# A hybrid encoder in fp32: a prologue ordered by channel tiles, and lower weight parts made by an accumulating transfer

## The chip, the cores and the metric

The kernel runs on one core of a Trainium2 chip. The metric is device time in microseconds (us) of one execution; a kernel's time is the median of its runs. The engines are TensorE (PE in the profile; its weight loads PEld), VectorE (DVE), ScalarE (ACT), GpSimd (POOL) and SyncE (SP). SP's queue issues most of the loads; GpSimd and ACT can issue transfers from queues of their own.

## The reference

Two layers, each a token mixer and a gated MLP, on x of shape (1, 256, 1024), all in float32:

```
for i in range(DEPTH):                                   # DEPTH = 2
    h = rms_norm(x, norm_mix_pre[i])
    u_hy, q, k, v, g_out, gate_lr, u_pool, gate_logits = split(h @ w_in[i])
    y_hy   = hyena_mixer(u_hy, ...)      # depthwise conv, long convolution by FFT, gating
    y_gla  = gla_mixer(q, k, v, g_out, gate_lr, ...)     # gated linear attention, both directions
    y_pool = pool_mixer(u_pool, ...)     # centred means over 2, 4, 8, 16, then a small matmul
    gates  = sigmoid(gate_logits)
    merged = gates[0] * (y_hy @ w_br_hyena[i]) + gates[1] * (y_gla @ w_br_gla[i]) \
           + gates[2] * (y_pool @ w_br_pool[i])
    x = x + rms_norm(merged @ w_out[i], norm_mix_post[i])
    h = rms_norm(x, norm_ffn_pre[i])
    a, b = split(h @ ffn_w_up[i])
    x = x + rms_norm((gelu(dwconv3(a)) * b) @ ffn_w_down[i], norm_ffn_post[i])
```

## The kernel before

**Precision by parts.** Each float32 operand of a matmul is written as an upper part, the value rounded to the format fp32r, and a lower part, the value minus the upper one. A product is three matmuls that add up in PSUM: upper by upper, upper by lower, lower by upper (`mm3`). For weights, ACT makes the upper part by a copy (`act`, line 106) and VectorE the lower one by a subtraction (`tt`, line 111).

**Weights.** They come in 71 chunks of 128x2048 a layer, with one small chunk between them, in a fixed order; chunk n is position n. `dma_next` loads the next chunk from SP's queue into one of three buffers (`raw`). `split_upper` and `split_lower` each turn half a chunk (128x1024) into a buffer of the pool `b` (37 buffers of 4 KB a partition). When the second half's lower part is asked for, the raw buffer is given back and the next load is written down. So the load of one chunk waits for the split of an earlier one. Some chunks ("paired", line 195) are loaded as two transfers. Chunks 10 to 23 are, in the first layer: the second chunk of the Hyena branch's x0, two of q, two of the pooling branch, two of k, then gates and projection of the pooling branch, and the first gate chunk of the Hyena branch.

**Order.** The program is written as a sequence of units, each a group of matmuls with its evictions; between units, `filler` splits further half chunks, up to three chunks ahead, as far as `b` has free buffers. Side generators (Hyena filters, attention heads, the pool products, which write `y_pl`) step in between. Tile's scheduler then orders the instructions on each engine by its own simulation of time. Every engine works through its own queue in order; a buffer's next user waits for the last user of what it held.

**The prologue** is under a manual schedule, in which the order of the code is kept. The token rows come in two tiles, x of tile 0 and of tile 1. For each: half of the squares on ACT, half on VectorE (`squares`), mean on VectorE and power -1/2 on GpSimd (`rstd_mean`), scaling (`scaled`), eight transposes (`turned`), then copies out of PSUM times the norm's gain, with upper and lower part (`gained`, by bank of two channel tiles). The gains in a column come from `grow`, a load of 8x128. `upper(k)` and `lower(k)` split a quarter of weight chunk 0, of 512 columns.

Of the kernel before, what the change touches and what calls it, by code (L numbers as in the profile page):

```python
# [16 lines left out]
ALU = mybir.AluOpType  # L17

P = 128
DEPTH = 2  # L20
L = 256
DM = 1024
# [62 lines left out]
def trunk(ctx: ExitStack, tc: tile.TileContext, a: dict, out: bass.AP):  # L85
    nc = tc.nc
# [8 lines left out]
    def f32(ap):  # L95
        return ap.bitcast(F32)
# [8 lines left out]
    def act(o, i, func=AF.Copy, **kw):  # L105
        ins = nc.scalar.activation(o, i, func, **kw)  # L106
        if func in TABLED:
            tc.stamp_issue_order_token(ins.ins, TOKEN)

    def tt(o, x, y, op):  # L110
        nc.vector.tensor_tensor(out=o, in0=x, in1=y, op=op)  # L111

    def stt(o, x, s, y, op0=ALU.mult, op1=ALU.mult):
        nc.vector.scalar_tensor_tensor(out=o, in0=x, scalar=s, in1=y, op0=op0, op1=op1)  # L114
# [42 lines left out]
    def load_x(t, parts):  # L157
        for s in parts:
            nc.sync.dma_start(xs[t][:, s], a["x"][t * P:(t + 1) * P, s])  # L159
# [8 lines left out]
    load_x(0, HALVES)  # L168
    gcol = cpool.tile([P, 8], F32, name="gcol")
    grow = cpool.tile([8, P], F32, name="grow")  # L170
    nc.sync.dma_start(grow[:], a["gains"][0, 0].rearrange("(k c) -> k c", c=P))


    order = []
# [5 lines left out]
    raws, wh, wl = {}, {}, {}  # L180
    state = {"dma": 0, "h": 0, "l": 0}

    def dma_next(parts=1, between=None):
        n = state["dma"]
        if n >= len(order):
            return
        kind, c = order[n]
        w = 2048 if kind == "w" else 512
        r = wpool.tile([P, w], F32, tag="raw", name=f"raw{n}")
        src = a["wts"][c] if kind == "w" else a["lrw"][c]  # L190
        if kind == "w" and c % NCHUNK in PAIRED:
            side = (c % NCHUNK - 16) % 3
            for m in range(2):
                src = a["wts"][c - side + m][:, side * 1024:(side + 1) * 1024].rearrange("p (k c) -> p k c", c=256)
                nc.sync.dma_start(r[:].rearrange("p (k c) -> p k c", c=512)[:, :, m * 256:(m + 1) * 256], src)
            parts = 0
        for m in range(parts):
            s = slice(m * w // parts, (m + 1) * w // parts)
            nc.sync.dma_start(r[:, s], src[:, s])
            if between is not None and m == 0:  # L200
                between()
        raws[n] = r
        state["dma"] = n + 1

    def split_upper():
# [13 lines left out]
        wl[n].append(big.get([P, 1024], F32R))  # L219
        act(wh[n][half][:], raws[n][:, half * 1024:(half + 1) * 1024])  # L220

    def split_lower():
        n, half = divmod(state["l"], 2)
        state["l"] += 1
        if order[n][0] == "lr":
            if half == 0:
                t = wh[n][0]
                r = raws[n][:].rearrange("p (k c) -> p k c", k=8)
                tt(t[:, :, 1, 0:32], r[:, :, 0:32], f32(t[:, :, 0, 0:32]), ALU.subtract)
        else:  # L230
            tt(wl[n][half][:], raws[n][:, half * 1024:(half + 1) * 1024], f32(wh[n][half][:]), ALU.subtract)
        if half == 1:
            del raws[n]
            dma_next()

    def split_half(lead=True):

        if state["l"] >= 2 * len(order):
            return
        if state["h"] == state["l"]:  # L240
            split_upper()
        if lead and state["h"] == state["l"] + 1 and state["h"] // 2 in raws and len(big.free) >= ahead["reserve"] + 4:
            split_upper()
        split_lower()
# [5 lines left out]
    def weights(n, at, width):  # L250

        half, at = divmod(at, 1024)
        return wh[n][half][:, at:at + width], wl[n][half][:, at:at + width]

    dma_next(2, lambda: load_x(1, [slice(0, DM)]))
    dma_next(2)
    dma_next()
    nc.sync.dma_start(vec[:], a["vec"])
# [123 lines left out]
    def rstd_mean(ss):  # L382

        r = cpool.tile([P, 1], F32, tag="rstd", bufs=4, name="rstd")
        e = cpool.tile([P, 1], F32, tag="mse", bufs=4, name="mse")
        tsc(e[:], ss[:, 0:1], ss[:, 1:2], EPS, ALU.add, ALU.add)
        nc.gpsimd.tensor_tensor(out=r[:], in0=e[:], in1=mhalf[:, 0:1], op=ALU.pow)  # L387
        return r
# [887 lines left out]
    def squares(t):  # L1276
        h, ss = big.get([P, DM]), ssq_tile()
        s0, s1 = HALVES
        act(h[:, s0], xs[t][:, s0], AF.Square, scale=1.0 / 32.0, accum_out=ss[:, 0:1])
        x = xs[t][:, s1]  # L1280
        nc.vector.scalar_tensor_tensor(out=h[:, s1], in0=x, scalar=1.0 / 1024.0, in1=x, op0=ALU.mult, op1=ALU.mult,
                                       accum_out=ss[:, 1:2])
        return h, ss

    def scaled(t, h, r):
        s0, s1 = HALVES
        act(h[:, s1], xs[t][:, s1], scale=r[:, 0:1])
        for s in (slice(s0.start, s0.start + 256), slice(s0.start + 256, s0.stop)):
            nc.vector.tensor_scalar_mul(h[:, s], xs[t][:, s], r[:])

    def turned(h):
        ps = [psm.get([P, 2, P]) for _ in range(4)]
        for k in range(8):
            nc.tensor.transpose(ps[k // 2][:, k % 2, :], h[:, k * P:(k + 1) * P], ident[:])  # L1294
        big.put(h)
        return ps

    def gained(t, half, ps, banks=(0, 1)):
        s = slice(t * P, (t + 1) * P)
        for bank in banks:  # L1300
            b = ps[half * 2 + bank]
            of = [(xt[0][half][:, k, s], xt[1][half][:, k, s], b[:, k % 2, :], gcol[:, half * 4 + k:half * 4 + k + 1])
                  for k in (2 * bank, 2 * bank + 1)]
            for xh, _, src, g in of:
                act(xh, src, scale=g)
            for xh, xl, src, g in of:
                stt(xl, src, g, f32(xh), ALU.mult, ALU.subtract)
            psm.put(b)
# [4 lines left out]
    def upper(k):  # L1313
        act(wh[0][k // 2][:, k % 2 * 512:(k % 2 + 1) * 512], raws[0][:, k * 512:(k + 1) * 512])

    def lower(k):
        s = slice(k % 2 * 512, (k % 2 + 1) * 512)
        tt(wl[0][k // 2][:, s], raws[0][:, k * 512:(k + 1) * 512], f32(wh[0][k // 2][:, s]), ALU.subtract)
# [14 lines left out]
    ps0 = turned(h0)  # L1333
# [2 lines left out]
    gained(0, 0, ps0, (0,))  # L1336
    upper(1)
    lower(1)
    gained(0, 0, ps0, (1,))
    h1, ss1 = squares(1)  # L1340
    r1 = rstd_mean(ss1)
    for k in (2, 3):
        upper(k)
        lower(k)
    scaled(1, h1, r1)
    del raws[0]
    dma_next()
    state["h"] = state["l"] = 2
# [158 lines left out]
```

## Time and profile before

| | |
|---|---|
| median of 3 runs | 886.82 us (885.36 to 887.30) |
| profiled execution | 885.61 us, of which the span is 883.8 us |
| TensorE busy | 871.4 us, 99% of the span |
| VectorE, ACT, GpSimd busy | 635.8, 511.8, 37.9 us |
| TensorE's granted clock | 0.998 |
| bytes moved by DMA | 163.46 MB, mean 185 GB/s |

The profile is that of one execution. A row of its timeline has the start in us from the span's start, the duration in us, the engine, the line of the kernel, the operation and its tiles (out<-in), and in brackets how long the engine was idle ahead of it and what ended that. L106 is the helper through which all ACT work goes, L111 that of VectorE's tensor-tensor operations, L120 that of matmuls; there one goes by the names of the tiles. A row of the waits has an engine, whom it waited for, the sum in us, how often, and the longest. A row by stretch of time has the stretch, its length, then the busy time of PE, PEld, DVE, ACT and POOL with the number of instructions, then the granted clock, the DMA engines' busy share and GB/s.

### The profile page before, as it was taken

The page shows a single profiled execution, that of the slowest core. Times are in us where ns is not written, and L with a number is a line of the kernel's source. Part 1 is how long each engine was busy: PE and PEld are TensorE (multiplying, and loading weights), DVE is VectorE, ACT ScalarE, POOL GpSimd, SP SyncE. Part 2 cuts the span into 40 slices and gives each one's busy share as a digit, 9 for nine tenths or more (in the row PEclk, how much of TensorE's full clock was granted, in tenths as well). Part 3 has the DMA queues.
Part 4 walks back from the last instruction along what each step waited for, and adds up shares of the span by engine and source line. Part 5 has one row for each costly group of instructions (what it writes and reads, how often), then busy time and mean ns, then how long its engine had stood idle before and what let it go on. Part 6 is the DMA issues. An engine that isn't in the chain of part 4 may idle for free.

```text
span 883.8 us, 13488 instructions
## 1 busy us (share of the span) xinstructions
PE 871.4 (99%) x5381; PEld 782.4 (89%) x5381; DVE 635.8 (72%) x925; ACT 511.8 (58%) x809; POOL 37.9 (4%) x86
## 2 busy tenths in 40 slices
PE   8999999999999999999999999999999999999996
PEld 6899987888888999998889999888888899999885
DVE  6899989766586798665288989876755967776612
ACT  6778757555365776554267855864543665555501
POOL 3000100000010000000010000000000000000000
PEclk9999999999999999999999999999999999999999
DMA  8863625746546436466349453455752674455501
GB/s 287 325 233 131 215 96 190 240 145 238 191 159 246 143 134 248 149 221 224 121 136 349 161 164 131 153 195 179 279 184 78 239 281 144 168 170 207 195 1 48
DMA packets 48143, 163.46 MB, mean 185 GB/s; under 512 B 3410, under 2 KB 29157, under 8 KB 33232
## 3 DMA queue, kind: packets, MB, share of 16 engines
q1 hardware_dynamic: 44080, 151.70, 48.9%
q0 software_dynamic: 4000, 10.90, 3.8%
q8 instruction: 42, 0.69, 0.3%
q14 instruction: 21, 0.17, 0.1%
HBM read 161.54 MB, written 1.05 MB: 184 GB/s over the span
## 4 chain that ended last, share of the span: by engine, by line
PE 95%; DVE 2%; DMA 1%; ACT 1%; issue 0%; SPq 0%; DVEq 0%; POOLq 0%; ACTq 0%
PE p L120 93%; DMA raw<-in_wts 1%; DVE b L111 1%; ACT b L106 1%; PE p L374 1%; PE p L1059 0%; PE p L1204 0%; PE p L775 0%; PE p L1021 0%; PE p L876 0%; DVE s L111 0%; PE p L1294 0%; SPq L159 0%; DVE x L114 0%; DVEq L1503 0%
## 5 line engine op out<-in xcount | busy, mean ns | idle before, releaser
L120 PE MATMUL p<-b,b 128*128 128x256 f32 (+2 forms) x5022 | 840.1, 328 | 4.0 <-DVE b L111 2.3
L120 PEld LDWEIGHTS p<-b,b 128*128 128x128 f32 x5022 | 739.8, 190 | 86.6 <-DVE b L111 3.7
L111 DVE TENSOR_TENSOR b<-raw,b 128x1024 fp32r<-128x1024 f32 (+2 forms) x288 | 342.3, 1208 | 114.1 <-ACT b L106 59.6
L106 ACT ACTIVATE b<-raw 128x1024 fp32r<-128x1024 f32 (+2 forms) x290 | 292.2, 1041 | 161.2 <-PE p L120 127.4
L111 DVE TENSOR_TENSOR b<-p,b 128x512 f32<-128x512 f32 (+2 forms) x72 | 45.8, 655 | 66.1 <-ACT s L106 44.6
L106 ACT ACTIVATE b<-p 128x512 f32<-128x512 f32 (+3 forms) x90 | 50.0, 571 | 64.2 <-PE p L120 38.7
L106 ACT ACTIVATE s<-p 128x256 f32<-128x256 f32 (+3 forms) x50 | 20.3, 415 | 69.0 <-PE p L120 68.7
L114 DVE SCALAR_TENSOR_TENSOR s<-p,vec,s 128x255 f32<-128x255 f32 x104 | 49.4, 479 | 6.5 <-ACT s L106 5.5
L106 ACT ACTIVATE s<-p,vec 128x256 f32<-128x256 f32 x52 | 28.8, 557 | 18.1 <-DVE s L114 15.5
L106 ACT ACTIVATE s<-s 128x512 f32<-128x512 f32 (+6 forms) x54 | 28.9, 535 | 11.5 <-DVE s L111 5.6
L111 DVE TENSOR_TENSOR b<-s,b 128x512 fp32r<-128x512 f32 (+1 forms) x42 | 28.6, 686 | 6.0 <-ACT b L106 6.0
L106 ACT ACTIVATE b<-s 128x512 fp32r<-128x512 f32 x38 | 23.5, 625 | 9.2 <-DVE s L111 9.1
L111 DVE TENSOR_TENSOR b<-b,b 128x512 f32<-128x512 f32 (+4 forms) x28 | 22.4, 802 | 3.6 <-ACT b L106 3.1
L111 DVE TENSOR_TENSOR b<-b,p 128x512 f32<-128x512 f32 x24 | 16.2, 683 | 7.7 <-PE p L120 7.3
L111 DVE TENSOR_TENSOR s<-s,p 128x512 f32<-128x512 f32 x22 | 15.0, 684 | 8.4 <-ACT s L106 8.0
L106 ACT ACTIVATE b<-b,s 128x128 f32<-128x128 f32 x64 | 20.5, 392 | 0.4 <-DVE s L700 0.4
L114 DVE SCALAR_TENSOR_TENSOR b<-p,vec,b 128x255 f32<-128x255 f32 (+1 forms) x40 | 19.1, 478 | 0.4 <-ACT b L106 0.3
L387 POOL TENSOR_TENSOR rstd<-mse,mhalf 128x1 f32<-128x1 f32 x16 | 9.3, 581 | 210.5 <-DVE mse L117 210.5
L106 ACT ACTIVATE b<-p,vec 128x256 f32<-128x256 f32 (+1 forms) x24 | 12.6, 527 | 9.0 <-PE p L120 7.1
L106 ACT ACTIVATE b<-b 1x512 f32<-1x512 f32 (+3 forms) x16 | 12.5, 783 | 4.2 <-DVE b L111 4.1
L106 ACT ACTIVATE s<-x 128x512 f32<-128x512 f32 x12 | 7.6, 634 | 11.6 <-DVE x L114 11.4
L111 DVE TENSOR_TENSOR s<-b,b 128x512 f32<-128x512 f32 x20 | 13.1, 685 | 1.5 <-PE p L120 1.4
(108 smaller groups left out, 310.7 us busy)
## 6 DMA issues: line engine op xcount, KB each, us to landing
raw<-in_wts SPq DMA_DIRECT2D x116, 1024.0 KB, 4.8
raw<-in_wts SPq DMA_DIRECT2D x52, 512.0 KB, 5.3
b<-in_gains POOLq DMA_DIRECT2D x7, 512.0 KB, 4.5
b<-in_dft POOLq DMA_DIRECT2D x4, 512.0 KB, 6.9
b<-in_gw POOLq DMA_DIRECT2D x2, 512.0 KB, 5.5
b<-in_fw POOLq DMA_DIRECT2D x2, 512.0 KB, 7.3
b<-in_decay POOLq DMA_DIRECT2D x2, 512.0 KB, 7.3
out<-x SPq DMA_DIRECT2D x4, 256.0 KB, 2.0
```

The lines of the kernel that those rows point to most:

```text
L106: ins = nc.scalar.activation(o, i, func, **kw)
L111: nc.vector.tensor_tensor(out=o, in0=x, in1=y, op=op)
L114: nc.vector.scalar_tensor_tensor(out=o, in0=x, scalar=s, in1=y, op0=op0, op1=op1)
L120: ins = nc.tensor.matmul(o, w, x, start=start, stop=stop).ins
L374: nc.tensor.transpose(ps[k // 4][:, k % 4, :], h[:, k * P:(k + 1) * P], ident[:])
L387: nc.gpsimd.tensor_tensor(out=r[:], in0=e[:], in1=mhalf[:, 0:1], op=ALU.pow)
```

## The change

Four edits:

- The load of `grow` is issued from ACT's queue instead of SP's.
- Chunk 0 is loaded in four quarters instead of two halves; x's tile 1 still goes when half of them are issued.
- In the prologue, the squares and the mean of x's tile 1 stand ahead of the second `gained` of tile 0; upper and lower part of quarter 3 stand around the scaling of tile 1.
- For the second half of chunks 10 to 23, `split_lower` has ACT write minus the raw weights, rounded to fp32r, and a transfer from GpSimd's queue add the raw weights to it.

```diff
-    nc.sync.dma_start(grow[:], a["gains"][0, 0].rearrange("(k c) -> k c", c=P))
+    nc.scalar.dma_start(grow[:], a["gains"][0, 0].rearrange("(k c) -> k c", c=P))
...
-            if between is not None and m == 0:
+            if between is not None and 2 * m + 2 == parts:
                 between()
...
+    def by_dma(n, half):
+        return 10 <= n < 24 and half == 1
+
     def split_lower():
...
+        elif by_dma(n, half):
+            src = raws[n][:, half * 1024:(half + 1) * 1024]
+            act(wl[n][half][:], src, scale=-1.0)
+            nc.gpsimd.dma_start(wl[n][half][:], src, accum_op=ALU.add)
         else:
             tt(wl[n][half][:], raws[n][:, half * 1024:(half + 1) * 1024], f32(wh[n][half][:]), ALU.subtract)
...
-    dma_next(2, lambda: load_x(1, [slice(0, DM)]))
+    dma_next(4, lambda: load_x(1, [slice(0, DM)]))
...
     lower(1)
-    gained(0, 0, ps0, (1,))
     h1, ss1 = squares(1)
     r1 = rstd_mean(ss1)
-    for k in (2, 3):
-        upper(k)
-        lower(k)
+    gained(0, 0, ps0, (1,))
+    upper(2)
+    lower(2)
+    upper(3)
     scaled(1, h1, r1)
+    lower(3)
     del raws[0]
```

In the rows of order below a name's numbers are the buffer's and the tile's own. VectorE's queue in the prologue of the kernel before, from the lower part of chunk 0's second quarter on (`b_5` to `b_8` are parts of chunk 0, `b_1` and `b_3` x's parts, `b_10` the rows of tile 1):

```order
L111 TENSOR_TENSOR b_7_111<-raw_81,b_5_109 128x512
L114 SCALAR_TENSOR_TENSOR b_3_105<-p_4_140,gcol,b_1_103 128x128 x2
L1281 SCALAR_TENSOR_TENSOR b_10_163,ssq<-x_68 128x512
L117 TENSOR_SCALAR mse<-ssq 128x1
L111 TENSOR_TENSOR b_8_112<-raw_81,b_6_110 128x512 x2
L1289 TENSOR_SCALAR b_10_163<-x_68,rstd 128x256 x2
L114 SCALAR_TENSOR_TENSOR b_3_105<-p_8_202,gcol,b_1_103 128x128 x2
```

And in the changed kernel:

```order
L111 TENSOR_TENSOR b_7_113<-raw_81,b_5_111 128x512
L1288 SCALAR_TENSOR_TENSOR b_10_161,ssq<-x_68 128x512
L117 TENSOR_SCALAR mse<-ssq 128x1
L114 SCALAR_TENSOR_TENSOR b_3_107<-p_4_142,gcol,b_1_105 128x128 x2
L111 TENSOR_TENSOR b_8_114<-raw_81,b_6_112 128x512
L1296 TENSOR_SCALAR b_10_161<-x_68,rstd 128x256 x2
L111 TENSOR_TENSOR b_8_114<-raw_81,b_6_112 128x512
L114 SCALAR_TENSOR_TENSOR b_3_107<-p_8_204,gcol,b_1_105 128x128 x2
```

The squares and mean of tile 1 now stand ahead of a gain step, and the last lower part of chunk 0 behind the scaling.

GpSimd's queue in the first layer, before, from the memsets behind the load of the inverse DFT (`b_110`) to the load of the attention's norm gains:

```order
L813 MEMSET b_110_1375 1x256
L814 MEMSET b_110_1375 1x64x2
L815 MEMSET b_110_1375 1x256
L914 MEMSET b_117_1422 128x2
L609 DMA gn<-in_glan 128x128
```

And now (raw_1106, 1257, 1152, 1348, 1515, 1591 and 1626 are chunks 17, 19, 18, 20, 21, 22 and 23):

```order
L820 MEMSET b_110_1385 1x256
L821 MEMSET b_110_1385 1x64x2
L822 MEMSET b_110_1385 1x256
L236 DMA b_106_1340<-raw_1106 128x1024
L921 MEMSET b_117_1432 128x2
L236 DMA b_124_1519<-raw_1257 128x1024
L236 DMA b_120_1449<-raw_1152 128x1024
L236 DMA b_129_1594<-raw_1348 128x1024
L236 DMA b_133_1630<-raw_1515 128x1024
L236 DMA b_138_1687<-raw_1591 128x1024
L236 DMA b_143_1734<-raw_1626 128x1024
L616 DMA gn<-in_glan 128x128
```

The transfers of chunks 17 to 23 stand in that stretch, chunk 19's ahead of chunk 18's. Those of chunks 10, 11, 13 and 12 stand ahead of the second DFT load, those of 14, 15 and 16 between the load of the pool weights and that of the inverse DFT.

ACT's queue before, from the first upper part of chunk 21 (raw_1504) to the second pool copy (`b_115`; `b_125` are copies out of PSUM for the Hyena products; raw_1579 is chunk 22):

```order
L106 ACTIVATE b_130_1609<-raw_1504 128x1024
L106 ACT_TABLE_LOAD
L106 ACTIVATE b_125_1511<-p_51_1512 128x512
L106 ACTIVATE b_115_1416<-p_50_1493,vec 128x256
L106 ACTIVATE b_135_1665<-raw_1579 128x1024
L106 ACTIVATE b_125_1511<-p_52_1552 128x512
L106 ACTIVATE b_132_1616<-raw_1504 128x1024
L106 ACTIVATE b_115_1416<-p_50_1493,vec 128x256
```

And now (`b_133` is minus the upper part of chunk 21's second half, raw_1515):

```order
L106 ACTIVATE b_130_1621<-raw_1515 128x1024
L106 ACTIVATE b_133_1630<-raw_1515 128x1024
L106 ACTIVATE b_115_1426<-p_50_1503,vec 128x256
L106 ACTIVATE b_132_1629<-raw_1515 128x1024
L106 ACT_TABLE_LOAD
L106 ACTIVATE b_125_1522<-p_51_1523 128x512
L106 ACTIVATE s_37_1609<-b_97_1214 1x512
L106 ACTIVATE s_42_1860<-b_49_445,s_7_447 128x128 x2
L106 ACTIVATE b_115_1426<-p_50_1503,vec 128x256
L106 ACTIVATE b_125_1522<-p_52_1563 128x512
```

Ahead of it, minus the upper part of chunk 19 stands right behind the first upper part of that chunk, and the second upper part comes later. The table load and the copies `b_125` moved behind both parts of chunk 21.

## The prediction

> **What bounds the kernel now.** I read the engines' busy time first, then the chain that ended last, then what TensorE (PE) waited for, then the table by stretch of time.
>
> ```profile
> PE 871.4 (99%) x5381; PEld 782.4 (89%) x5381; DVE 635.8 (72%) x925; ACT 511.8 (58%) x809; POOL 37.9 (4%) x86
> ...
> PE 95%; DVE 2%; DMA 1%; ACT 1%; issue 0%; SPq 0%; DVEq 0%; POOLq 0%; ACTq 0%
> ```
> ```profile
> PE p L120 <- DVE b L111: 2.3, 2, 1.8
> PE p L120 <- ACT b L106: 1.8, 2, 1.4
> PE p L120 <- DVE rmask L260: 1.2, 1, 1.2
> PE p L1294 <- DVE b L1289: 0.4, 1, 0.4
> ```
> ```profile
> 60.00:90.00 30.00, 30.00 (x237) 29.02 (x237) 29.90 (x62) 25.60 (x54) 1.87 (x6) 1.00 0.32 125
> 90.00:120.00 30.00, 30.00 (x232) 29.04 (x231) 27.13 (x47) 20.07 (x40) 2.51 (x8) 1.00 0.49 159
> 120.00:150.00 30.00, 28.22 (x127) 23.09 (x126) 27.08 (x40) 18.96 (x30) 0.00 (x0) 1.00 0.53 175
> ```
>
> TensorE is the bound. All its waits (us in total, times, longest) add up to 5.7 us: the start, and one wait of 1.8 us, which takes TensorE to 28.22 of 30 us in the last stretch. VectorE (DVE) is busy 29.90 of 30 us from 60 to 90 us, yet TensorE is at 30.00 there: taking work off VectorE shortens nothing by itself. What can be gained is a piece of the start, and the wait of 1.8 us; what can be lost is any cover that keeps TensorE dense.
>
> **The start.** Rows of the timeline (start, duration, then the work; in brackets the idle time before it), the first from the chain:
>
> ```profile
> 2.06 5.95 DMA raw<-in_wts
> ...
> x<-in_x SPq DMA_DIRECT2D x1, 512.0 KB, 6.8
> ...
> 2.46 0.43 SPq L159 DMA_DIRECT2D x<-in_x  x1
> ...
> 8.04 0.63 ACT L106 ACTIVATE b<-raw 128x512 fp32r<-128x512 f32 x1 [1.37 <-DMA raw<-in_wts]
> ...
> 10.95 0.68 DVE L1281 SCALAR_TENSOR_TENSOR b<-x 128x512 f32<-128x512 f32 x1
> ...
> 11.75 0.21 DVE L117 TENSOR_SCALAR mse<-ssq 128x1 f32<-128x1 f32 x1
> 11.88 1.28 DVE L111 TENSOR_TENSOR b<-raw,b 128x512 fp32r<-128x512 f32 x2
> 13.08 0.61 DVE L1289 TENSOR_SCALAR b<-x,rstd 128x256 f32<-128x256 f32 x2
> ...
> 12.04 0.93 POOL L387 TENSOR_TENSOR rstd<-mse,mhalf 128x1 f32<-128x1 f32 x1 [6.12 <-DVE mse L117]
> ...
> 13.48 1.20 PE L1294 MATMUL p<-ident,b 128*128 128x128 f32 x8 [0.37 <-DVE b L1289]
> ```
>
> The second half of x lands at 2.46 + 6.8 = 9.26 us, but VectorE squares its part of it only at 10.95, behind two lower parts and two gain steps. From there the mean (11.75), the power on GpSimd (12.04 to 12.97), the scaling (13.08) and the transposes (13.48) follow. The change loads the first weight chunk in quarters, with x between the second and the third. The bytes ahead of x are the same but for the 4 KB of gains, which go to ACT's queue, ahead of its table load; I cost both at nothing, since x's landing is set by the bytes queued before it. The first quarter lands earlier than 8.02 us: ACT's idle 1.37 us shrinks, and upper and lower parts 0 and 1 are out of the way by x's landing. Squares then run from about 9.3 to 10.0, mean by 10.2, power by 11.15. On VectorE there follow the gain step (two, 0.6) and lower part 2 (0.69, half of the row of 1.28), whose upper part ACT makes by 11.1; so VectorE reaches the scaling at about 11.8 instead of 13.08. The gain of lower part 3's move behind the scaling is in this. Transposes at 12.3 instead of 13.48: **1.2 us** gained. Bounds: 0.3 if x or the third quarter lands a microsecond later, since four smaller transfers stand in the same queue; 1.9 if scaling waits for the power alone (11.15 against 13.08).
>
> **Fourteen lower parts by a transfer.** Chunks 10 to 23 are meant, the second half of each.
>
> ```profile
> L111 DVE TENSOR_TENSOR b<-raw,b 128x1024 fp32r<-128x1024 f32 (+2 forms) x288 | 342.3, 1208 | 114.1 <-ACT b L106 59.6
> L106 ACT ACTIVATE b<-raw 128x1024 fp32r<-128x1024 f32 (+2 forms) x290 | 292.2, 1041 | 161.2 <-PE p L120 127.4
> ...
> raw<-in_wts SPq DMA_DIRECT2D x116, 1024.0 KB, 4.8
> ...
> b<-in_gains POOLq DMA_DIRECT2D x7, 512.0 KB, 4.5
> ```
> ```profile
> b<-in_gw POOLq DMA_DIRECT2D x1, 512.0 KB, 3.6
> ```
> ```profile
> b<-in_dft POOLq DMA_DIRECT2D x1, 512.0 KB, 8.5
> ```
>
> VectorE loses 14 x 1.21 = 16.9 us, ACT gains 14 x 1.04 = 14.6 us. Neither sum is on the path, but ACT runs in order: at 25.60 of 30 us from 60 to 90 us, four or five more parts fill it. I cost that at nothing there, since ACT has 9.9 us free in the next stretch, and price the order of its work below, where it matters.
>
> The accumulating transfer has no row. The nearest are plain loads of 512 KB from the same queue (last column: us from issue to landing): 3.6 with the DMA engines quiet, 4.5 at the median of the seven gains, 8.5 for one at 76 us. It also reads its destination; from 512 KB (3.6) to 1024 KB (4.8, on SP's queue) another 512 KB took 1.2 us. So I take 4.5 + 1.2 = **5.7 us**, with ends 3.6 (the second read is free) and 8.5 + 1.2 = 9.7 us. I choose near the median because SP's row below has no weight load issued between chunk 20's pair (from 103.47) and chunk 21's pair (its second at 121.77), where the price decides.
>
> The Trainium skill, "DMA: Bandwidth & Descriptors", section "Anatomy of one DMA — SWDGE (gpsimd) path", gives about 2.0 us plus the bytes at 436 GB/s; its page "Collectives: The Full Stack", section "The bandwidth ceiling: the fold count and why AG ≠ RS ≠ AR", says that an add in a transfer costs a second source read rather than cycles. By both, as an estimate, the price is 2.0 + 1.2 + 1.2 = 4.4 us, and the sum below would be +0.55 instead of +1.85; the plain rows here (4.5 at the median, against 3.2 by the formula) speak for more.
>
> **Where it meets the path.** A raw buffer used to be free when VectorE had made the second lower half; now it is free when the transfer has landed. Three raw buffers stand behind this, so each of SP's loads 13 to 27 starts later against its split, and the transfers queue on GpSimd, in whose order a DFT load, the pool weights, the inverse-DFT loads and memsets stand behind transfers that wait for ACT. I cost that at nothing: each is held by a negation of 1.04 us or two, and TensorE works on other branches meanwhile. Most loads have cover too. The place without is the wait of 1.8 us: chain, then ACT's rows there, then the rows ahead of it.
>
> ```profile
> 121.77 5.37 DMA raw<-in_wts
> ...
> 127.16 1.07 ACT b L106
> ...
> 128.25 1.23 DVE b L111
> ...
> 131.68 4.69 DVE b L111 x6
> ...
> 136.41 3.70 PE p L120 x15
> ```
> ```profile
> 128.24 1.28 ACT L106 ACT_TABLE_LOAD   x1
> 129.53 0.60 ACT L106 ACTIVATE b<-p 128x512 f32<-128x512 f32 x1
> 130.03 0.47 ACT L106 ACTIVATE b<-p,vec 128x256 fp32r<-128x256 f32 x1
> ...
> 131.81 1.07 ACT L106 ACTIVATE b<-raw 128x1024 fp32r<-128x1024 f32 x1
> 132.76 0.48 ACT L106 ACTIVATE b<-p,vec 128x256 fp32r<-128x256 f32 x1
> 133.12 0.62 ACT L106 ACTIVATE s<-b 1x512 f32<-1x512 f32 x1
> 133.64 0.68 ACT L106 ACTIVATE s<-b,s 128x128 f32<-128x128 f32 x2
> ```
> ```profile
> 103.47 18.80 SPq L195 DMA_DIRECT2D raw<-in_wts  x4
> ...
> 110.83 0.47 ACT L106 ACTIVATE b<-p,vec 128x256 fp32r<-128x256 f32 x1 [2.13 <-PE p L120]
> ...
> 116.23 2.96 ACT L106 ACTIVATE b<-raw 128x1024 fp32r<-128x1024 f32 x3 [2.78 <-PE p L120]
> ```
>
> Chunk 21's load is a pair: SP's row ends at 122.27, its last issue is the chain's 121.77, and the one ahead of it, as long, starts near 121.35. It lands at 127.14; ACT's upper part, VectorE's lower part, the Hyena products and then the lower part of chunk 20 follow, and TensorE waits for that last one until 136.41. In the new order the buffer for chunk 21 comes from chunk 19's transfer. ACT makes minus the upper part of chunk 19 right behind that chunk's first upper part, which waits for TensorE to free a buffer until 116.23. With TensorE 1.2 earlier, the negation ends between 112.2 (right behind the pool copy at 110.83 less 1.2, its 0.47 and two parts) and 117.1 (behind 116.23 less 1.2 and two parts). I take 116.1, near the upper end, since buffers come free with TensorE's progress and the new form holds them no shorter. Plus 5.7 the load is issued at 121.8. To keep pace with a TensorE that is 1.2 earlier it had to go at 120.15: **1.65 us** late. The ends of the transfer's price give −0.45 and 5.65.
>
> Then ACT's order behind chunk 21's first upper part. Before, the first copy out of PSUM for the Hyena products started 2.4 us after that part (129.53 against 127.16), the second pool copy 5.6 us after it. Now minus the upper part of chunk 21 (1.05), a pool copy (0.47) and chunk 21's second upper part (1.07) stand between it and the table load: the first copy moves back by some 2.1 us, and the second pool copy, for which TensorE's pool products wait, by 0.6 (a short row and the two 128x128 pieces also pass it, another copy and a chunk's upper part leave). I take **1.4 us**, the middle, since VectorE has the lower part and a product of older data to do meanwhile; ends 0 and 2.1.
>
> **The sum**: −1.2 + 1.65 + 1.4 = +1.85 us on the profiled execution's 885.61, which lies 1.2 under the median of the runs, 886.82. So 888.7 us by the runs.
>
> **The rivals.** *Not slower: a quick transfer.* At 3.6 us chunk 21's load goes at 119.7, 0.45 ahead of need. If ACT's new order is also hidden (0), the wait shrinks from 1.8 to 1.35 and the start's 1.2 stays: −1.65, and −2.35 with the start's 1.9, so 884.5 to 885.2. The mechanism is the early release of one raw buffer; it decides from a landing under 4.05 us after the issue. The 3.6 row speaks for it, the second operand against it.
>
> *Slow transfers.* The plain load at 76 us took 8.5 us with VectorE full (29.90 of 30) and the DMA engines at 0.32. At 9.7 us the sum is −1.2 + 5.65 + 1.4 = +5.85, so 892.7, and transfers queued behind each other (chunks 19, 18 and 20 follow in one row on GpSimd's queue) could make a second place like it: 897. TensorE would then wait already for chunks' own lower halves. For it: VectorE is at 27 of 30 us from 90 to 150 us too. Against: it loses the fourteen products there, and the same queue brought the gains in 4.5. The Trainium skill, "SBUF — State Buffer", section "SBUF: two separate sides", says that VectorE's two-port operations keep GpSimd from writing descriptors, so that such transfers seem blocked; by that rule the 8.5 would be the price wherever VectorE is full. The trace shows the slow load but not its cause.
>
> *The start gives nothing.* If the quarters delay x by as much as the order saves (gain 0.3), the loss is 2.75: 889.6.
>
> **Chances.** The likeliest case 0.48, its own range 886.5 to 890.5; the quick transfer 0.22; slow transfers 0.20; no gain at the start 0.10. A change under 0.2%, 1.77 us, is about what a measurement of this kernel cannot tell from none. The likeliest case lies at that edge (888.6) and is split 0.24 same, 0.24 slower; the quick one 0.15 faster, 0.07 same; slow transfers all slower; the last 0.07 same, 0.03 slower; rounded: faster 0.15, same 0.38, slower 0.47. The range, 885.2 to 896, leaves out the better half of the quick case and the end of the slow one.
>
> **What the profile after would show.** Right: transposes near 12.3; fourteen transfers from raw to b on GpSimd's queue at about 5.7 us each; chunk 21's load issued at 121 to 122.5; TensorE's wait near 133 us grown from 1.8 to about 4.8 us, with chunk 21's landing behind it, and TensorE dense elsewhere; VectorE 17 us lighter, ACT 15 heavier. Wrong: landings near 3.6 or 9; new waits between 60 and 130 us, of TensorE for b from a transfer; transposes still at 13; or the wait gone although chunk 21 comes as late, which would say that VectorE's queue made it.

## The result: 1.2% slower, and the profile after

| | before | after |
|---|---|---|
| median of runs | 886.09 us (4 runs, 884.21 to 887.30) | 896.26 us (4 runs, 895.36 to 897.77) |
| span of the profiled execution | 883.8 us | 895.0 us |

The ratio of the times is 1.0119 (95% interval 1.0105 to 1.0133): 10.2 us lost, where 1.9 were forecast; 896.26 lies just above the range (885.2 to 896.0). The profiled executions differ by 11.2 us, and two views of the kernel after hold that sum within 0.3 us. Its engines' busy time and TensorE's waits:

```profile
PE 875.9 (98%) x5381; PEld 784.8 (88%) x5381; DVE 622.1 (70%) x911; ACT 523.4 (58%) x823; POOL 49.7 (6%) x100
...
PE p L120 <- DMA b<-raw: 7.9, 3, 4.5
PE p L120 <- ACT b L106: 3.1, 2, 2.0
PE p L120 <- DVE rmask L267: 1.2, 1, 1.2
PE p L1301 <- DVE b L1296: 0.5, 1, 0.5
```

The waits are 12.7 us against 5.7, which is 7.0 more; and TensorE is busy 4.5 us longer with the same 5381 matmuls. The timeline shows where the waits lie; these are the rows from 10 us on that TensorE idled before:

```profile
10.94 1.52 PE L120 MATMUL p<-b,b 128*128 128x512 f32 x3 [1.12 <-ACT b L106]
...
134.37 15.82 PE L120 MATMUL p<-b,b 128*128 128x512 f32 x62 [4.49 <-DMA b<-raw]
...
152.21 6.36 PE L120 MATMUL p<-b,b 128*128 128x512 f32 x26 [2.01 <-ACT b L106]
159.42 3.02 PE L120 MATMUL p<-b,b 128*128 128x512 f32 x12 [0.85 <-DMA b<-raw]
168.68 6.46 PE L120 MATMUL p<-b,b 128*128 128x512 f32 x25 [2.60 <-DMA b<-raw]
```

Between 14 and 129 us TensorE is as dense as before. What it waits for at 134 shows the chain: chunk 18's transfer, issued at 125.45 and 8.88 us long, and behind it, as that chunk's raw buffer comes free, the load of chunk 22 (issued at 122.44 before), which takes 8.03:

```profile
125.45 8.88 DMA b<-raw
134.33 0.02 SPq L199
134.35 0.03 issue
134.38 8.03 DMA raw<-in_wts
```

The longer busy time is the clock. By stretch of time (its last three columns are the granted clock, the DMA engines' share and GB/s):

```profile
126.00:130.00 4.00, 3.88 (x20) 2.94 (x18) 3.35 (x7) 1.75 (x4) 1.16 (x2) 1.00 0.74 156
130.00:134.00 4.00, 0.00 (x0) 0.00 (x0) 0.97 (x1) 2.06 (x3) 0.00 (x0) 1.00 1.11 265
134.00:138.00 4.00, 3.63 (x9) 2.88 (x10) 4.00 (x7) 3.62 (x6) 0.86 (x1) 0.57 1.01 237
138.00:142.00 4.00, 4.00 (x19) 3.31 (x18) 2.27 (x6) 1.44 (x5) 0.00 (x0) 1.00 1.00 235
```

Behind the wait the clock is 0.57 for 4 us: 9 matmuls where the next stretch has 19. The Trainium skill, "TensorE: Matmul & The Clock Gate", section "HAM oscillation — how this bites in real kernels", warns of idle gaps of more than some 3.4 us on TensorE; the trace agrees for this gap of 4.49 us. The kernel before, whose longest wait is 1.78 us, has 1.00 there. But the wait of 2.60 us, shorter than that, was followed by a dip as deep:

```profile
168.00:170.00 2.00, 1.32 (x3) 1.13 (x4) 2.00 (x4) 0.00 (x0) 0.00 (x0) 0.57 1.05 329
170.00:172.00 2.00, 2.00 (x6) 1.54 (x6) 1.22 (x2) 0.00 (x0) 0.00 (x0) 0.57 1.09 329
```

In the new prologue the transposes of tile 1 start at 12.25 instead of 13.48 us:

```profile
12.25 1.91 PE L1301 MATMUL p<-ident,b 128*128 128x128 f32 x8
```

The eight took 1.91 instead of 1.20 us, at a granted clock of 0.50 from 12 to 14 us. Their starts are those of single executions: the old prologue has them at 12.35 us in the run of the transfers alone, the new one at 11.60 to 12.60 in the other runs with it. The profiled executions of all runs below with this prologue have 1.00 from 8 to 16 us, and the one with the old prologue and the transfers 0.82, so that dip isn't the new order's own; what makes it stays open. As an estimate by the share of the clock that is missing, it costs 1.7 us (0.18, 0.50 and 0.17 of 2 us each from 10 to 16 us), and the two dips behind waits 1.7 us each (0.43 of 4 us); together that is 5.1 us, where the busy time grew by 4.5.

### The profile page after: what moved, and what is told of

It is laid out like the page before. It is cut to its first block, busy times and chain, and to the rows that moved or that the text cites. A ratio compares the mean times of both kernels' runs of the same rounds, so it can differ in the third digit from the quotient of the medians.

```text
span 895.0 us, 13551 instructions
## 1 busy us (share of the span) xinstructions
PE 875.9 (98%) x5381; PEld 784.8 (88%) x5381; DVE 622.1 (70%) x911; ACT 523.4 (58%) x823; POOL 49.7 (6%) x100
## 4 chain that ended last, share of the span: by engine, by line
PE 80%; DMA 4%; ACT 1%; issue 1%; DVE 0%; DVEq 0%; POOLq 0%; ACTq 0%; SPq 0%
PE p L120 79%; DMA b<-raw 2%; DMA raw<-in_wts 2%; ACT b L106 1%; PE p L381 1%; PE p L1211 0%; PE p L1066 0%; PE p L1028 0%; ACT s L106 0%; PE p L782 0%; PE p L883 0%; DVE x L114 0%; DVEq L1511 0%; POOLq L1511 0%; DVE s L114 0%
## 5 line engine op out<-in xcount | busy, mean ns | idle before, releaser
L111 DVE TENSOR_TENSOR b<-raw,b 128x1024 fp32r<-128x1024 f32 (+2 forms) x274 | 325.4, 1207 | 136.0 <-ACT b L106 92.5
L106 ACT ACTIVATE b<-raw 128x1024 fp32r<-128x1024 f32 (+1 forms) x304 | 306.1, 1041 | 174.8 <-PE p L120 108.1
L236 POOL DMA_DIRECT2D b<-raw x14 | 12.2, 873 | 105.6 <-ACT b L106 49.2
L164 POOL DMA_DIRECT2D b<-in_gains x7 | 3.9, 552 | 235.0 <-PE p L120 123.2
```

Source lines behind the costliest of these rows:

```text
L164: eng.dma_start(g[:], bass.AP(src.tensor, src.offset + (i * 4 + j) * DM, [[0, P], [1, DM]]))
L236: nc.gpsimd.dma_start(wl[n][half][:], src, accum_op=ALU.add)
```

## The experiments

Times are medians, ratios are against the kernel before on the same chip (885.74, 885.46 and 885.51 us in the three groups).

**The prologue alone.** `return 10 <= n < 24 and half == 1` in `by_dma` becomes `return False`.

> The prologue's three edits alone; all lower parts on VectorE as before. Theory A (the transfers cost the whole loss, the new prologue is a gain): 0.5 to 1.4 us faster than before, transposes of the second tile at 12.3 us, and the wait of 1.8 us near 133 us as before. Rival (the new prologue's drop of TensorE's granted clock to 0.50 from 12 to 14 us is part of the loss): no faster than before, transposes early but slow.

884.74 us, ratio 0.9986 (0.9975 to 0.9997): 1.0 us gained, inside theory A's bounds. TensorE busy is 871.4 us as before. The clock is 1.00 from 8 to 16 us, so this run doesn't show what the dip costs. The transposes run at 12.51, and the wait near 133 us is there:

```profile
135.33 16.79 PE L120 MATMUL p<-b,b 128*128 128x512 f32 x72 [1.73 <-DVE b L111]
```

**The transfers alone.** The kernel before with `by_dma` and its branch in `split_lower`, nothing else.

> The fourteen transfers alone, with the prologue of before. Theory A: 10 to 12 us slower than before (the change's 10.2 plus the prologue's gain), with TensorE waits for b from a transfer near 130, 159 and 168 us. Rival (only both edits together collide, since the prologue shifts TensorE against the loads): under 5 us slower.

898.39 us, 1.0143 (1.0130 to 1.0156): 12.7 slower, a little over theory A's 10 to 12, with TensorE's waits of 4.45, 0.86 and 2.52 us on transfers at 135, 159 and 168. The loss is the transfers'. It is 2.5 us more than the changed kernel's; the prologue alone gains 1.0, and the rest lies within the intervals.

**Negation on ACT, addition on VectorE.**

```diff
             act(wl[n][half][:], src, scale=-1.0)
-            nc.gpsimd.dma_start(wl[n][half][:], src, accum_op=ALU.add)
+            tt(wl[n][half][:], src, f32(wl[n][half][:]), ALU.add)
```

> The changed kernel, but VectorE adds the raw weights to what ACT made, instead of a transfer: ACT keeps the fourteen negations, GpSimd and the DMA engines lose the fourteen transfers. Theory A (the transfer's landing is the loss): within 2 us of before. Rival (ACT's fourteen extra parts and its new order are the loss): 5 us or more slower than before.

886.15 us, 1.0003 (0.9994 to 1.0012): 1.4 slower than the prologue alone, so ACT's fourteen parts and the order around them are a small share, and the transfer the large one. TensorE waits 1.00 and 1.58 us between 132 and 136 us here, 0.85 more than with the prologue alone.

**A plain transfer.** One operand read instead of two; the lower parts of the fourteen halves are then the raw weights.

```diff
-            nc.gpsimd.dma_start(wl[n][half][:], src, accum_op=ALU.add)
+            nc.gpsimd.dma_start(f32(wl[n][half][:]), src)
```

> The changed kernel with a plain transfer of raw to b from the same queue instead of the accumulating one: one operand read instead of two; the lower parts of those fourteen halves are then the raw weights. If the second operand makes the transfers long (5.7 was taken as 4.5 + 1.2), their median falls from 6.8 to about 5.5 us and the time to 3 to 7 us over before. Rival (what makes them long is other transfers beside them and the issue): median within 0.5 us of 6.8 and the time within 2 us of the changed kernel's 896.

889.59 us, 1.0043 (1.0029 to 1.0058), and the median transfer is shorter than either theory had it. The changed kernel's row of transfers, then this one's:

```profile
b<-raw POOLq DMA_DIRECT2D x14, 512.0 KB, 6.8
```
```profile
b<-raw POOLq DMA_DIRECT2D x14, 512.0 KB, 3.8
```

Of the 11.5 us between the prologue alone and the changed kernel, by differences of medians (the kernel before differs by up to 0.6 us between the groups): 1.4 ACT, 3.4 a plain transfer in VectorE's place, 6.7 the accumulation in it. The prologue's dip of some 1.7 us, which this run's profiled execution doesn't have, can be part of the 6.7.

**Which chunks.** Transfers for `10 <= n < 18` and for `18 <= n < 24`, and all but `n == 18`.

> The new prologue, with transfers for chunks 10 to 17 alone. Theory A (a transfer costs only where TensorE uses the half, or SP's next load, soon after; that is at chunks 18 to 23): within 1.5 us of the prologue alone, so 884 to 886.5 us, no wait of TensorE on a transfer. Rival (every transfer delays the chain of raw buffers a little, and the loss adds up from chunk 10 on, chunk 20's load going at 115.7 instead of 103.5 us): 3 us or more slower than before, with the wait near 133 us grown.

885.82 us, 1.0005 (0.9996 to 1.0014): 1.1 us over the prologue alone, inside theory A's bounds, with no wait on a transfer. But the rival's mechanism is there: chunk 20's load goes at 114.82 us, and TensorE's waits at 131 to 137 are 2.8 us together instead of 1.73.

> The new prologue, with transfers for chunks 18 to 23 alone. Theory A: nearly the whole loss, 7 to 11 us slower than before. Rival (the delay adds up from chunk 10 on): under 5 us slower, since chunk 20's load goes at about 103 us as before.

890.85 us, 1.0064 (1.0050 to 1.0078): 5.4 slower, between the two forecasts. Over the prologue alone, the two parts cost 1.1 and 6.1 us, the whole 11.5: the last 4.3 come of both, and neither theory is right by itself. Here chunk 20's load went at 106.72 and chunk 22's at 126.44 us, with all fourteen at 115.70 and 134.38; I take the late loads that the first eight leave behind for the 4.3, but no run shows that apart. With the last six alone TensorE waits on no transfer: its waits of 1.97 us at 132.82 and 2.04 us at 137.61 are on ACT.

> The changed kernel with chunk 18's half back on VectorE; thirteen transfers. TensorE's first wait (4.49 us, ended by chunk 18's transfer, 125.45 to 134.33) goes. Theory A (own lower half late): 4 to 7 us faster than the changed kernel, since the drop of the granted clock behind that wait goes too. Rival (the raw buffers' chain is late anyway, and another half takes its place): under 2.5 us faster, with a wait of 3 us or more at the same place on something else.

890.63 us, 1.0058 (1.0044 to 1.0072): 5.6 faster than the changed kernel for one half given back, as theory A had it. The wait of 4.49 became three, none over 2 us, and the clock stays at 1.00 behind them (134 to 142 us, against 0.57 and 1.00):

```profile
132.54 1.65 PE L120 MATMUL p<-b,b 128*128 128x512 f32 x6 [1.69 <-ACT b L106]
135.28 1.21 PE L120 MATMUL p<-b,b 128*128 128x512 f32 x4 [1.09 <-ACT b L106]
137.73 16.61 PE L120 MATMUL p<-b,b 128*128 128x512 f32 x71 [1.24 <-DVE b L111]
```

**The queue on GpSimd.** In the changed kernel chunk 17's transfer waits behind memsets that wait for the inverse-DFT loads:

```profile
109.54 0.30 POOL L820 MEMSET b<- 1x256 f32 x1 [4.44 <-DMA b<-in_ih]
109.91 0.20 POOL L821 MEMSET b<- 1x128 f32 x1
110.26 0.30 POOL L822 MEMSET b<- 1x256 f32 x1
110.88 0.91 POOL L236 DMA_DIRECT2D b<-raw  x1 [0.31 <-issue]
```

The edit is `nc.vector.memset` for those three.

> The changed kernel with the three memsets on the inverse-DFT buffer moved from GpSimd to VectorE; every queue's order is else the same. Chunk 17's transfer, issued at 110.88 behind memsets that waited until 109.54 and 110.21 for those loads, though its negation was done at 108.72, goes 2.0 us earlier, and with it chunk 20's load and chunk 18's negation behind it on ACT. If that queue is a link of the chain: TensorE's wait of 4.49 us shrinks by 1 to 2.2 us and the time falls by 1 to 3 us. Rival (another wait holds chunk 20's load): within 0.8 us of the changed kernel.

895.87 us, 1.0114 (1.0095 to 1.0132): the rival holds. The transfer went at 107.78 and chunk 20's load at 113.89 instead of 115.70, but TensorE waited 3.85 us at the same place, and the median moved by 0.4 us, less than the interval. In that chain two microseconds at this link are not two at its end.

**Four raw buffers.** `bufs=4` for raw and 35 buffers for `b`, the same bytes: in the changed kernel, and with the prologue alone.

> The changed kernel with four raw buffers and 35 in b. If the loss is that SP's loads wait for transfers that hold raw buffers, most of it goes: 4 us or more faster than the changed kernel's 896. Rival (TensorE waits for the halves that the transfers write, whenever the weights came): under 2.5 us faster.

893.84 us, 1.0089 (1.0072 to 1.0105): 2.4 us better, under the rival's bound of 2.5. TensorE now waits 4.95 us at 163 for the half of a transfer that took 9.19 beside four weight loads. Holding the raw buffers is the smaller part; the transfer's own length is the larger.

> The prologue alone, with four raw buffers instead of three and 35 instead of 37 buffers in the pool b (the same bytes). If chunk 21's late load sets the wait of 1.7 us, it goes earlier and the wait shrinks: 1 to 2 us faster than the prologue alone, 883 to 884 us. Rival (the pool b, not raw, is what runs out): no faster than the prologue alone, or slower.

884.33 us, 0.9987 (0.9977 to 0.9997): not to be told from the prologue alone, and outside the 883 to 884 us of the theory. The theory is right about the place, TensorE being busy 30.00 of 30 us from 120 to 150, and still little is gained. The waits:

```profile
PE p L120 <- DVE rmask L267: 1.2, 1, 1.2
PE p L1301 <- DVE b L1296: 1.2, 1, 1.2
PE p L381 <- DVE b L114: 0.9, 1, 0.9
PE p L120 <- ACT b L106: 0.7, 1, 0.7
PE p L120 <- DVE b L111: 0.2, 1, 0.2
```

Of the 1.73 us, 1.1 come back as waits at 262 (0.9) and 464 us (0.2), 0.3 in the prologue. This execution and that of the prologue alone span 882.2 and 882.3 us.

**One transfer alone**, with the new prologue: `return n == 20 and half == 0`.

> The new prologue with one transfer alone, for the first half of chunk 20, whose lower part VectorE made last ahead of the wait of 1.7 us in the kernel before, though its upper part is made by 119 us. If that order on VectorE is the wait, it shrinks by 1 us or more: 1 to 2 us faster than the prologue alone, 882.5 to 884 us. Rival (chunk 21's late landing sets it whatever VectorE does last): as the prologue alone, 884.7.

887.97 us, 1.0031 (1.0020 to 1.0043), slower than both forecasts: it told nothing of VectorE's order, because ACT reached the negation only at 131 us, behind chunk 21's parts, and the transfer, 4.6 us long with nothing beside it, became the wait:

```profile
132.24 0.92 POOL L236 DMA_DIRECT2D b<-raw  x1 [22.00 <-ACT b L106]
```
```profile
136.86 16.51 PE L120 MATMUL p<-b,b 128*128 128x512 f32 x64 [3.31 <-DMA b<-raw]
```

**The transfer by itself**, in a kernel that makes nothing else: after each negation, the transfer alone, beside a load, beside VectorE, and two in a row.

> Not the encoder: a kernel with transfers of 512 KB from GpSimd's queue alone, one after the other, its output being x plus what is left over. In turn, twice, accumulating and plain: nothing beside; one weight load of 1024 KB from SP's queue beside; eight products on VectorE beside; two transfers back to back. Theory A (the DMA engines are shared, and an accumulating transfer gives way to a load): accumulating 4.5 us alone and with VectorE busy, 8 us or more beside a load, the load itself 6 us or more; plain 2.9 alone, 5 to 7 beside a load. Rival (VectorE keeps GpSimd from writing the transfer's list): 7 us or more with VectorE busy, under 5.5 beside a load.

The issues of five stretches: accumulating alone (74 to 80.5 us), beside a load (80.5 to 90.5), beside VectorE (90.5 to 97, busy 5.71 of 6.5 us); then plain alone (44 to 48.5) and beside a load (48.5 to 56.5). Last column: us to landing.

```profile
low<-raw POOLq DMA_DIRECT2D x1, 512.0 KB, 4.5
...
wide<-in_wts SPq DMA_DIRECT2D x1, 1024.0 KB, 6.3
low<-raw POOLq DMA_DIRECT2D x1, 512.0 KB, 8.6
...
low<-raw POOLq DMA_DIRECT2D x1, 512.0 KB, 4.5
...
low<-raw POOLq DMA_DIRECT2D x1, 512.0 KB, 2.9
...
wide<-in_wts SPq DMA_DIRECT2D x1, 1024.0 KB, 5.7
low<-raw POOLq DMA_DIRECT2D x1, 512.0 KB, 6.8
```

The times are theory A's in each case, and the rival's in none: VectorE's products beside it change nothing (4.5 either way), one load beside it adds 4 us, to the plain transfer too. In the other turn the numbers were within 0.25 us of these, but for the very first transfer, which ran beside the loads of the start (6.3 us). In the changed kernel the fourteen transfers spread the same way: 4.5 to 4.7 us where less moved (at 51.9, 72.3, 110.9 and 154.9), 10.4, 8.9, 8.2, 9.9 and 8.9 beside weight loads (at 56.3, 125.5, 128.7, 134.2 and 159.7), the other five 5.0 to 7.7.

## Why the prediction was wrong, point by point

| step | forecast | shown |
|---|---|---|
| gain of the prologue | −1.2 us, transposes at 12.3 | −1.0 (prologue alone), transposes at 12.25 |
| ACT's new order and parts | +1.4, ends 0 and 2.1 | +1.4 in all (addition on VectorE), 0.85 of it at 132 to 136 us |
| minus the upper part of chunk 19 ends | 116.1 | 118.51 |
| a transfer | 5.7 us, ends 3.6 and 9.7 | chunk 19's 5.2; 4.5 alone, 8.6 beside a load; median 6.8 |
| chunk 21's load issued | 121.8 | 124.97 |
| wait near 133 us | 4.8 us, behind chunk 21's landing | 4.49, behind chunk 18's own transfer |
| other waits on transfers and late loads | none | 5.5 us (2.01 + 0.85 + 2.60) |
| TensorE's clock behind waits | not in the sum | some 3.4 us of longer busy time (estimate) |

**The step that failed is the path: the transferred halves, and all loads but one, stood in the sum at nothing.** The forecast ran a single wait through chunk 19's transfer and chunk 21's load. Of the transfers queued on GpSimd and of the other late loads it said "I cost that at nothing", since "TensorE works on other branches meanwhile". On the path that it did price, the 5.7 us nearly held. The rows are chunk 19's negation, its transfer, the last lower part ahead of chunk 21's load, and that load:

```profile
117.45 1.06 ACT L106 ACTIVATE b<-raw 128x1024 fp32r<-128x1024 f32 x1 [0.38 <-PE p L120]
...
118.82 0.88 POOL L236 DMA_DIRECT2D b<-raw  x1 [6.91 <-ACT b L106]
...
123.72 1.23 DVE L111 TENSOR_TENSOR b<-raw,b 128x1024 fp32r<-128x1024 f32 x1 [3.71 <-ACT b L106]
...
124.97 0.37 SPq L195 DMA_DIRECT2D raw<-in_wts  x1
```

The transfer took 5.2 us and landed at 124.0. But the negation ended 2.4 us later than forecast, behind TensorE, and the load waited last for the lower part on VectorE, until 124.95. So it came 3.2 us late against the forecast, for other reasons than the price. And TensorE didn't wait for it: it stopped at 129.88 for chunk 18's own transfer, issued at 125.45 and 8.88 us long. At the 4.5 us of a transfer alone that one would have landed at 129.95, as an estimate, and next to nothing of this wait would be left. With chunk 18's half back on VectorE the kernel was 5.6 us faster, though other waits, 4.0 us together, came in that place.

**The price was read off the old trace, without the transfers that the change itself moves.** I took 5.7 "because SP's row below has no weight load issued between chunk 20's pair (from 103.47) and chunk 21's pair". That row is of the kernel before. In the changed kernel the held raw buffers move chunk 20's load to 115.70 (107.20 with the prologue alone), and chunk 21's goes at 124.97, half a microsecond ahead of chunk 18's transfer. The change made its own contention. The right price was not one number with two ends but two: 4.5 us alone, below mine, and near my upper end beside a load. The 4.4 worked out from the Trainium skill, as cited there, was nearer to the first than my 5.7.

The trace before had the second price, and I misread it. I put the 8.5 us of the load at 76 us down to VectorE, with "the DMA engines at 0.32", and said that the trace doesn't show its cause. That 0.32 is the mean from 60 to 90 us. From 70 to 90 us in half microseconds (each digit a busy share in tenths) the DMA engines are nearly full from 75 to 83 us, and two weight loads ran beside it:

```profile
DMA  0000000000948989979899999500000000000000
...
raw<-in_wts SPq DMA_DIRECT2D x2, 1024.0 KB, 6.8
b<-in_dft POOLq DMA_DIRECT2D x1, 512.0 KB, 8.5
```

**The place was right and the waiter was wrong.** The wait is where the sum put it, and by luck of about the forecast length, but TensorE waited for a transferred half itself. I had that only in the rival on slow transfers ("TensorE would then wait already for chunks' own lower halves"), and that rival is what came: it gave 892.7 and, with a second place, 897. I gave it 0.20 and cut the range at 896. Its cause was named wrongly, as VectorE's load: with VectorE's products running the transfer took 4.5 us as without. No run here shows at work the rule cited there of the Trainium skill, "SBUF — State Buffer", section "SBUF: two separate sides"; the eight products are subtractions, and no other operation of VectorE was tried by itself beside a transfer.

**Two terms were missing.** I stopped at the first wait; the load of chunk 22, 12 us later than before, and the transfers of the last two chunks made three more. And every long wait was costed at its length, while the clock behind it made it longer: TensorE's busy time is 875.9 us against 871.4 with the prologue alone, and by the estimate above about two thirds of the difference lie behind waits. The rest is the dip in the prologue, which no step of the forecast and no mechanism shown here explains.

**What held**: the bound, the prologue's gain within 0.2 us, ACT's order in size, and that VectorE's parts, 16.9 us lighter (its busy time fell by 13.7), buy nothing where TensorE is dense. The forecast's own path is in the runs too: with the last six chunks alone, the chain to TensorE's wait of 2.04 us runs through chunk 21's load at 122.60 and ACT's parts, table load and copies behind it.

## What to carry to other kernels

Work taken off an engine that isn't waited for gains nothing, and work given to a transfer that holds two buffers until it lands can cost more than its engine time: here 1.2 us of VectorE became 4.5 to 10 us of holding. Price a new transfer beside the transfers as the change will place them, not as the old trace has them, and with its own operands counted. A wait that TensorE didn't have before is dearer than its length, if it is long enough to lower the granted clock.

## What the runs showed of the hardware

- An accumulating transfer of 512 KB from SBUF to SBUF took 4.5 us alone, a plain one 2.9; its issue on GpSimd took about 0.87 instead of 0.54 us. Beside a load of 1024 KB both took 4 us more, and the load took 6.3 and 5.7 us. Two accumulating ones back to back took 4.6 and 6.2 us.
- The clock fell also behind waits under 3 us each that stood close together. With transfers for the first eight chunks TensorE was idle 2.04 us and, just behind, 0.37; the clock, the last column but two, was 0.88 and then 0.70:

```profile
134.00:138.00 4.00, 2.11 (x6) 1.48 (x7) 4.00 (x5) 3.06 (x7) 0.00 (x0) 0.88 0.00 0
138.00:142.00 4.00, 4.00 (x14) 3.13 (x14) 3.98 (x10) 2.40 (x5) 0.00 (x0) 0.70 0.83 248
```

With all but chunk 18, idle 1.69, 1.09 and 1.24 us within seven microseconds, it stayed at 1.00.

- Single waits of 2.01 us (changed kernel, 152 us) and 2.17 us (plain transfer, 140 us) left the clock at 1.00; those of 2.52 us (transfers alone, 169 us) and 2.60 us (changed kernel, 169 us) were followed by 0.53 and 0.57. What decides between them no run shows.
